# Squares of the input norm on other engines, high parts of softmax weights on ScalarE, and state space blocks moved by other transfers, in a one-core decoder trunk

## The chip, the core and the metric

The kernel runs on one core of a Trainium2 chip. The core has a matrix engine (TensorE, PE in the rows; its weight loads are PEld), VectorE (DVE), ScalarE (ACT), GpSimd (POOL), and SyncE (SP), which in this kernel issues every transfer. Each engine works through its own list of instructions in the order in which the program was built; an instruction that waits holds up all that stands behind it on that engine.

The metric is the device time of one execution in microseconds. Before the change it is 2130.84 us, the median of 3 runs (2130.14 to 2133.14).

## The reference, cut to what matters

```python
def layer(x, mem):                        # x: 1024 tokens x 1024 channels, float32
    h = rmsnorm(x, norm_mix)
    fq, fk, fv, ff, su, hq, hf, hi, hg, gl = split(h @ w_in)
    y_fox = fox_attention(q, k, v, log_f)     # 8 heads x 64, causal softmax with a forget bias
    y_s5  = s5_mixer(su, ...)                 # 32 groups x 16 channels, 64 complex states each,
                                              # gelu, then z * sigmoid(z @ w_glu + b_glu)
    y_hg  = hgrn2_mixer(hq, hf, hi, hg)       # 4 heads, chunks of 64
    merged = sum(sigmoid(gl)[b] * (y_b @ w_branch[b]) for y_b in (y_fox, y_s5, y_hg))
    x = x + merged @ w_out
    x = x + cross_attention(rmsnorm(x), rmsnorm(mem))    # 4 heads, 256 memory tokens
    x = x + swiglu(rmsnorm(x))
```

## The kernel before

Activations lie transposed: channels on the 128 partitions, the 1024 tokens along the row. A float32 product is made of three float32r matmuls: each operand is split into a high part (`xh`, `wh`, `yh`, `zh`, made by ScalarE) and the low remainder (`xl`, `wl`, `yl`, `zl`, made by VectorE), and PE runs high x high, low x high, high x low. A block of weights is loaded raw (`wr`), split into `wh` and `wl`, and used for one projection of 1024 tokens (two halves of 512, PSUM tile `pj`).

The stages, in the order of time:

- Start (0 to about 60 us). `load_x` loads the eight blocks `xk` of x, splits them into `xh` and `xl` and sums their squares for the input norm: blocks with an even number are squared on ScalarE and added on VectorE (`acc`), blocks with an odd number are squared and added on GpSimd (`accg`, which shows as `sq` in the rows). `run` meanwhile feeds PE with the projections `su0` and `su1`; one VectorE instruction merges `accg` into `acc`, and `row_scale` sums over the partitions on PE (`rs`). The outputs `su0` to `su3` are the input of the state space part; `su_evac` scales them and stores each to `su_d` in HBM.
- S5 (about 95 to 320 us). Eight blocks `o` of four groups. `s5_prep` loads a block's input as `s5u`, `s5_prep2` and `s5_body` build the operands (`kcs`, written by VectorE, is the last one) and run the matmuls (`s5y`), `s5_out` applies the gelu and stores to `sz_d`. `s5_main` runs the four steps for different blocks in turn; between two steps a planner puts projection matmuls (`pj`) on PE, `S5_W[lag] * S5_US` microseconds of them by its own count.
- FoX (about 320 to 600 us). Sixteen units (head pair `p`, half of the queries, head `h`). For each key block `j`, PE makes scores `st`, ScalarE the exponentials `pf`, GpSimd their high part `pt` (first half of the tile) and the running sum `facc`, VectorE the low part `pt` (second half), PE the product with the values `pv`. `fox_pre` prepares the next unit in between: the row maxima `mx`, and from them in `chain` the tile `mc` (GpSimd copies a constant into it, VectorE writes the two columns of the maxima), which `rows` transposes on PE (`mt`). When both heads of a pair have ended, `sums` splits `facc` into `ah` and sums it on PE (`sm`). `later(us, fn)` puts it that many planned microseconds of PE behind.
- HGRN2 (about 600 to 980 us), then the merge. For each branch, `gates(b, y)` multiplies eight output blocks by a gate that comes back from HBM (`gate`, from `gz_d`). First gate stage 0 (FoX), while the last HGRN2 head ends (`hoT`, stored to `hy_d`); then `glu` (the product z @ w_glu, on `zt`, loaded from `sz_d`, split into `zh` and `zl`); then `gates(1)` (S5) and `gates(2)` (HGRN2, whose inputs `load_parts` reads back from `hy_d` as `ldy` and splits into `yh` and `yl`).
- Output projection, cross attention and SwiGLU follow; the change does not touch them.

What sets the order: every instruction gets a rising priority when the program is written, and the scheduler orders each engine's list by it and by dependence. `ahead(n, fn)` gives the instructions of `fn` a priority that is n steps earlier. `drive` and `pump` write projection matmuls between the steps of a stage. Tiles such as `gate`, `wr`, `zt` and `ldy` come from one arena of equal slots, and a load waits until a slot is free.

Of the kernel before, what the change touches and what calls it, by code (L numbers as in the profile page):

```python
# [10 lines left out]
F32 = mybir.dt.float32  # L11
# [42 lines left out]
S5_W = (1.0, 0.6, 1.0, 1.2)  # L54
# [19 lines left out]
MIX_US = 8.5  # L74
EPS = 1e-6
# [118 lines left out]
class Trunk:  # L194
# [280 lines left out]
    def load_x(self):  # L475

        nc = self.nc
        self.xh = [self.u(f"xh{k}", F32R) for k in range(KB)]
        self.xl = [self.u(f"xl{k}", F32R) for k in range(KB)]
        acc, accg = self.u("acc"), self.u("sq")  # L480
# [4 lines left out]
        def square(k, xk):  # L485
            if k % 2 == 0:
                self.sq_add(xk, acc, k, eng=nc.vector)
                return
            sq = accg if k == 1 else self.u("sq")
            self.mul(sq, xk, xk, nc.gpsimd)  # L490
            if k > 1:
                self.add(accg, accg, sq, nc.gpsimd)

        last = None
        for k in range(KB):
            xk = self.u("xk")
            cuts = [slice(0, NT)] if k else [slice(0, 512), slice(512, NT)]
            if k == 0:
                nc.sync.dma_start(out=raw[:, 0:2], in_=ap[:, 0:2])
            for c in cuts:  # L500
                nc.sync.dma_start(out=xk[:, c], in_=self.io["xT"][k][:, c])
            if k == 0:
                nc.sync.dma_start(out=raw[:, 2:], in_=ap[:, 2:])
                self.w_load(1)
                self.split(raw[:, 0:2], hi[:, 0:2], lo[:, 0:2])
            for c in cuts:
                self.split_gain(xk[:, c], self.par("norm_mix", k), self.xh[k][:, c], self.xl[k][:, c])
            if k == 0:
                self.split(raw[:, 2:], hi[:, 2:], lo[:, 2:])
                del self.wraw[0]  # L510
                self.w_prep(1)
            else:
                square(k - 1, last)
            last = xk
        self.w_load(2)
        square(KB - 1, last)
        return acc, accg

# [164 lines left out]
    def fox_pre(self, un):  # L683
# [32 lines left out]
        def chain():  # L716
# [3 lines left out]
            mc = self.sp.tile([P, 4, 16], F32, tag="mc", name="mc")  # L720
            mh = self.sp.tile([P, 4], F32R, tag="mh", name="mh")
            self.nc.gpsimd.tensor_copy(out=mc, in_=self.ohc[:, hd].unsqueeze(1).to_broadcast([P, 4, 16]))
# [3 lines left out]
            st["mc"] = mc  # L726
# [11 lines left out]
        return out + [chain, rows]  # L738

    hi_pool = (0, 1, 2, 3)  # L740

    def fox_main(self):
# [11 lines left out]
        for ui, un in enumerate(units):  # L754
# [17 lines left out]
            for j in range(nj):  # L772
# [12 lines left out]
                if j % 4 in self.hi_pool:  # L785
                    self.ts(pt[:, 0, q0:512], pr, 1.0, 0.0, ALU.mult, ALU.add, self.nc.gpsimd)
                else:
                    self.act(pt[:, 0, q0:512], pr, AF.Copy)
# [29 lines left out]
    def fox_out(self, un, o, acc):  # L818
# [26 lines left out]
        if h == 1:  # L845
            self.later(2.0, sums)
# [31 lines left out]
    def su_evac(self, i):  # L878
        st = {}

        def f(ps, c, last):
# [7 lines left out]
            self.nc.sync.dma_start(out=self.su_d[128 * i:128 * i + 128], in_=t)  # L889
# [205 lines left out]
    def s5_prep(self, o):  # L1095
# [108 lines left out]
    def s5_out(self, o):  # L1204
# [21 lines left out]
        qv = q.rearrange("p (g c) -> p g c", g=4)  # L1226
# [103 lines left out]
    def run(self, stop=None):  # L1330
        nc = self.nc
        self.su_d = self.dp.tile([512, 8, 128], F32, name="su_d")
        self.fy_d = self.dp.tile([4, P, NT], F32, name="fy_d")
        self.hy_d = self.dp.tile([4, P, NT], F32, name="hy_d")
        self.sz_d = self.dp.tile([512, 8, 128], F32, name="sz_d")
# [16 lines left out]
        xs = acc = accg = None  # L1352
# [988 lines left out]
```

## Time and profile before

| | |
|---|---|
| median of 3 runs | 2130.84 us |
| the profiled execution's own time | 2138.17 us |
| its span on the core | 2136.1 us |
| mean granted TensorE clock | 0.992 |
| PE busy | 2079.2 us (97% of the span) |
| VectorE busy | 1521.9 us (71%) |
| ScalarE busy | 814.8 us (38%) |
| GpSimd busy | 608.2 us (28%) |

The profile is of one execution. Its rows come in a few views: the page (busy times of the engines, the chain that ended last), the waits of an engine, groups of instructions by line, a timeline of an engine (start in us, duration in us, line, what it did, and in brackets the idle time ahead and whose result ended it), and windows (busy times and the mean granted clock of PE in a stretch; 1.00 is 2.4 GHz, 0.50 is 1.2 GHz).

### The profile page before, as it was taken

What the parts mean: (1) busy time and instruction counts of PE and PEld (TensorE: products, weight loads), DVE (VectorE), ACT (ScalarE), POOL (GpSimd) and SP (SyncE); (2) the same over time, 40 slices, a digit from 0 to 9 for tenths busy, and PEclk for the clock granted to TensorE, in tenths of its full rate; (3) what the DMA queues carried; (4) which work ended last, traced back from release to release, by engine and by line L of the source; (5) the groups of instructions that cost most, each with busy time, mean ns of one, the idle gap of its engine ahead of it and who ended that gap; (6) DMA issues with size and microseconds to landing.
All of it is one profiled execution on the core that took longest, in us unless ns stands there. A gap on an engine that the chain in (4) does not pass through costs nothing.

```text
span 2136.1 us, 26862 instructions
## 1 busy us (share of the span) xinstructions
PE 2079.2 (97%) x10044; PEld 1706.7 (80%) x10044; DVE 1521.9 (71%) x2229; ACT 814.8 (38%) x1268; POOL 608.2 (28%) x551
## 2 busy tenths in 40 slices
PE   7998999999999999999999999999999999999999
PEld 5887777776788878888778888878788888888887
DVE  8887898888854566545675567656897778775772
ACT  4113345545531123215434445444533333344441
POOL 4281204454543223221722100011032324221320
PEclk9999999999999999999999999999999999999999
DMA  4332221110213233235554523334232322248582
GB/s 163 137 104 74 51 75 32 40 50 30 70 46 124 73 109 123 74 99 196 194 192 154 201 92 106 119 117 135 74 120 98 124 99 99 103 150 282 189 281 99
DMA packets 121042, 250.94 MB, mean 117 GB/s; under 512 B 15816, under 2 KB 53704, under 8 KB 120912
## 3 DMA queue, kind: packets, MB, share of 16 engines
q1 hardware_dynamic: 120912, 249.23, 34.2%
q8 instruction: 79, 1.29, 0.3%
q14 instruction: 51, 0.42, 0.1%
HBM read 184.83 MB, written 63.18 MB: 116 GB/s over the span
## 4 chain that ended last, share of the span: by engine, by line
PE 59%; DVE 4%; DMA 1%; ACT 1%; issue 0%; SPq 0%; DVEq 0%; ACTq 0%
PE fp L228 27%; PE pj L228 26%; PE hs L228 2%; PE xo L228 1%; PE xs L228 1%; PE rs L228 1%; PE ho L228 0%; DVE t L246 0%; DVE tl L246 0%; DVE gate L246 0%; DMA gate<-gz_d 0%; DVE yl L246 0%; DMA wr<-xv 0%; DMA ldy<-hy_d 0%; PE xt L233 0%
## 5 line engine op out<-in xcount | busy, mean ns | idle before, releaser
L228 PE MATMUL pj<-xl,wh 128*128 128x512 f32 x784 | 315.5, 406 | 4.7 <-DVE xl L258 4.6
L228 PE MATMUL pj<-xh,wh 128*128 128x512 f32 x784 | 313.3, 405 | 6.7 <-ACT xh L243 5.8
L228 PE MATMUL pj<-xh,wl 128*128 128x512 f32 x784 | 311.7, 401 | 0.0
L246 DVE TENSOR_TENSOR wl<-wr,wh 128x1024 fp32r<-128x1024 f32 (+2 forms) x138 | 170.4, 1236 | 58.5 <-ACT wh L243 56.2
L228 PE MATMUL fp<-th,wc 128*128 128x512 f32 x640 | 206.9, 389 | 0.0
L228 PE MATMUL fp<-hh,wc 128*128 128x512 f32 x644 | 191.4, 389 | 0.0
L228 PEld LDWEIGHTS pj<-xh,wh 128*128 128x128 f32 x784 | 149.2, 190 | 40.0 <-ACT xh L243 6.1
L228 PEld LDWEIGHTS pj<-xl,wh 128*128 128x128 f32 x784 | 148.5, 190 | 37.4 <-DVE xl L258 7.1
L228 PEld LDWEIGHTS pj<-xh,wl 128*128 128x128 f32 x784 | 149.1, 190 | 30.8 <-issue 1.9
L228 PE MATMUL fp<-fx,wc 128*128 128x512 f32 x720 | 172.9, 389 | 0.0
L243 ACT ACTIVATE wh<-wr 128x1024 fp32r<-128x1024 f32 (+2 forms) x138 | 131.8, 957 | 76.8 <-DMA wr<-w_in 50.3
L228 PEld LDWEIGHTS fp<-fx,wc 128*128 128x128 f32 x720 | 135.2, 188 | 28.0
L228 PEld LDWEIGHTS fp<-hh,wc 128*128 128x128 f32 x644 | 120.9, 188 | 25.0
L228 PEld LDWEIGHTS fp<-th,wc 128*128 128x128 f32 x640 | 120.2, 188 | 24.9
L246 DVE TENSOR_TENSOR wc<-wr,wc 128x512 fp32r<-128x512 f32 (+1 forms) x116 | 108.5, 954 | 31.4 <-ACT wc L243 31.4
L246 POOL TENSOR_TENSOR dm<-dm 128x256 f32<-128x256 f32 (+1 forms) x96 | 79.5, 828 | 179.9 <-DMA dm<-w_dn 163.0
L246 POOL TENSOR_TENSOR acc<-acc,sq 128x512 f32<-128x512 f32 (+1 forms) x18 | 30.7, 1706 | 340.5 <-ACT sq L243 340.4
L228 PE MATMUL fp<-tl,wc 128*128 128x512 f32 x320 | 124.6, 389 | 0.7 <-DVE tl L246 0.7
L246 DVE TENSOR_TENSOR pt<-pf,pt 128x512 fp32r<-128x512 f32 (+1 forms) x96 | 94.4, 985 | 40.2 <-POOL pt L262 39.9
L246 POOL TENSOR_TENSOR fc<-fc,fs 128x512 f32<-128x512 f32 x40 | 58.0, 1449 | 216.2 <-ACT fs L243 216.2
L228 PE MATMUL fp<-hl,wc 128*128 128x512 f32 x280 | 108.9, 389 | 0.0
L262 POOL TENSOR_SCALAR pt<-pf 128x512 fp32r<-128x512 f32 (+1 forms) x96 | 67.7, 706 | 139.0 <-ACT pf L243 127.8
(427 smaller groups left out, 4862.3 us busy)
## 6 DMA issues: line engine op xcount, KB each, us to landing
wr<-w_in SPq DMA_DIRECT2D x48, 512.0 KB, 4.8
wr<-w_gu SPq DMA_DIRECT2D x44, 512.0 KB, 4.1
hr<-hb_d SPq DMA_DIRECT2D x35, 512.0 KB, 5.4
hb_d<-fc SPq DMA_DIRECT2D x44, 256.0 KB, 2.1
gz_d<-gz SPq DMA_DIRECT2D x20, 512.0 KB, 2.9
dm<-w_dn SPq DMA_DIRECT2D x20, 512.0 KB, 5.6
ws_d<-dm SPq DMA_DIRECT2D x20, 512.0 KB, 3.3
gate<-gz_d SPq DMA_DIRECT2D x20, 512.0 KB, 6.4
```

The costliest lines, as they stand in the source:

```text
L228: self.nc.tensor.matmul(out, lhsT, rhs, start=start, stop=stop)
L243: self.nc.scalar.activation(out=out, in_=in_, func=f, **kw)
L246: return (eng or self.nc.vector).tensor_tensor(out=out, in0=a, in1=b, op=op)
L262: (eng or self.nc.vector).tensor_scalar(out=out, in0=a, scalar1=s1, scalar2=s2, op0=op0, **kw)
```

## The change

Five edits.

1. Input norm: all eight squares go to ScalarE, after all the splits, and the seven additions to VectorE behind the last `xl`. GpSimd has no part in it, and the merge is gone.
2. `su_d` and `sz_d` get another layout, by blocks. `s5_prep` loads a block with one transfer of 128 x 512 in place of eight, `s5_out` stores with one in place of eight. On the other sides `su_evac` stores with eight transfers in place of one (4 to 32 in all), and each `zt` is loaded with eight in place of one (4 to 32). In all SP issues 703 transfers in place of 759.
3. `S5_W`: the planner puts 1.6 in place of 1.0 of its units behind `s5_prep` and 0.6 in place of 1.2 behind `s5_out`.
4. FoX: the high part of all 96 exponentials is a ScalarE copy; the constant of `mc` is copied when a unit is built; `chain` is written with a priority 40 steps ahead; `sums` comes 6.0 in place of 2.0 planned microseconds later.
5. `load_parts` is stepped during `gates(1)`: the inputs of `gates(2)` are loaded and split between the gates of `gates(1)`.

PE runs the same 9467 instructions.

```diff
-S5_W = (1.0, 0.6, 1.0, 1.2)
+S5_W = (1.6, 0.6, 1.0, 0.6)
+SUM_AT = 6.0
+AH_MAX = 40
@@ load_x
-            else:
-                square(k - 1, last)
-            last = xk
         self.w_load(2)
-        square(KB - 1, last)
-        return acc, accg
+        for k, xk in enumerate(xs):
+            self.sq_add(xk, acc, k, eng=nc.vector)
+        return acc
@@ fox_pre, build
+            mc = st["mc"] = self.sp.tile([P, 4, 16], F32, tag="mc", name="mc")
+            self.nc.gpsimd.tensor_copy(out=mc, in_=self.ohc[:, hd].unsqueeze(1).to_broadcast([P, 4, 16]))
@@ fox_pre, chain
-            self.nc.gpsimd.tensor_copy(out=mc, in_=self.ohc[:, hd].unsqueeze(1).to_broadcast([P, 4, 16]))
@@ fox_pre, end
-        return out + [chain, rows]
-    hi_pool = (0, 1, 2, 3)
+        return out + [lambda: self.ahead(AH_MAX, chain), rows]
@@ fox_main
-                if j % 4 in self.hi_pool:
-                    self.ts(pt[:, 0, q0:512], pr, 1.0, 0.0, ALU.mult, ALU.add, self.nc.gpsimd)
-                else:
-                    self.act(pt[:, 0, q0:512], pr, AF.Copy)
+                self.act(pt[:, 0, q0:512], pr, AF.Copy)
@@ sums
-            self.later(2.0, sums)
+            self.later(SUM_AT, sums)
@@ su_evac
-            self.nc.sync.dma_start(out=self.su_d[128 * i:128 * i + 128], in_=t)
+            for n in range(8):
+                self.nc.sync.dma_start(out=self.su_d[2 * i + n // 4][:, :, n % 4].rearrange("s h c -> h s c"),
+                                       in_=t[16 * n:16 * n + 16])
@@ s5_prep
-        for s in range(8):
-            nc.sync.dma_start(out=U[16 * s:16 * s + 16],
-                              in_=self.su_d[64 * o:64 * o + 64, s].rearrange("(g h) c -> h g c", g=4))
+        nc.sync.dma_start(out=ut[:, 0:512], in_=self.su_d[o].rearrange("s h g c -> (s h) (g c)"))
@@ s5_out
-        for t in range(8):
-            nc.sync.dma_start(out=self.sz_d[64 * o:64 * o + 64, t].rearrange("(g h) c -> h g c", g=4),
-                              in_=qv[16 * t:16 * t + 16])
+        nc.sync.dma_start(out=self.sz_d[o].rearrange("t h g c -> (t h) (g c)"), in_=q)
@@ run
-                self.stt(acc, accg, 1.0 / 1024.0, acc, ALU.mult, ALU.add)
@@ run, loads of zt
-            self.nc.sync.dma_start(out=z, in_=self.sz_d[128 * i:128 * i + 128].rearrange("p t c -> p (t c)"))
+            zv = z.rearrange("p (t c) -> p t c", t=8)
+            for n in range(8):
+                self.nc.sync.dma_start(out=zv[16 * n:16 * n + 16],
+                                       in_=self.sz_d[2 * i + n // 4][:, :, n % 4].rearrange("t h c -> h t c"))
@@ run, gates
-        self.filler("gate1", self.gates(1, ys))
+        yh = []
+        self.filler("gate1", self.gates(1, ys, self.load_parts([self.hy_d[h] for h in range(4)], yh)))
-        self.filler("gate2", self.gates(2, self.load_parts([self.hy_d[h] for h in range(4)])))
+        self.filler("gate2", self.gates(2, yh))
@@ gates
             yield from self.gate(b, ob, y)
+            if side is not None:
+                next(side, None)
```

Where the order of the engines' lists differs. First VectorE at the start, before the change, from the split of the third last block of x on (`xl` is the low part of x, `acc` the sum of squares):

```order
L258 SCALAR_TENSOR_TENSOR xl_91<-xk,parT,xh_83 128x1024
L246 TENSOR_TENSOR acc<-acc,sq 128x1024
L258 SCALAR_TENSOR_TENSOR xl_92<-xk,parT,xh_84 128x1024
L258 SCALAR_TENSOR_TENSOR xl_93<-xk,parT,xh_85 128x1024
L246 TENSOR_TENSOR acc<-acc,sq 128x1024
L258 SCALAR_TENSOR_TENSOR acc<-sq,acc 128x1024
L441 CAST crr<-cr 128x384
L246 TENSOR_TENSOR wl<-wr,wh 128x1024
L258 SCALAR_TENSOR_TENSOR acc<-rs,cst,acc 128x512
```

The same place on VectorE after the change:

```order
L260 SCALAR_TENSOR_TENSOR xl_91<-xk,parT,xh_83 128x1024
L260 SCALAR_TENSOR_TENSOR xl_92<-xk,parT,xh_84 128x1024
L260 SCALAR_TENSOR_TENSOR xl_93<-xk,parT,xh_85 128x1024
L248 TENSOR_TENSOR acc<-acc,sq 128x1024 x6
L443 CAST crr<-cr 128x384
L248 TENSOR_TENSOR acc<-acc,sq 128x1024
L248 TENSOR_TENSOR wl<-wr,wh 128x1024
L260 SCALAR_TENSOR_TENSOR acc<-rs,cst,acc 128x512
```

The additions that stood between the splits stand behind them, and there are seven in place of three and a merge.

PE at the end of a FoX head pair, before the change (the place of the sums `sm` at 508.6 to 512.2 us in the timeline; the last `pv` of the pair are 128 wide):

```order
L228 MATMUL pv<-pt,vs 128x128
L228 MATMUL pj<-xh_83,wh 128x512
L228 MATMUL pj<-xl_91,wh 128x512
L228 MATMUL pj<-xh_83,wl 128x512
L228 MATMUL pj<-xh_84,wh 128x512
L228 MATMUL pj<-xl_92,wh 128x512
L228 MATMUL pj<-xh_84,wl 128x512
L228 MATMUL pj<-xh_85,wh 128x512
L228 MATMUL pj<-xl_93,wh 128x512
L228 MATMUL pj<-xh_85,wl 128x512
L228 MATMUL pj<-xh_78,wh 128x512
L228 MATMUL sm<-ah,crr 8x512 x3
```

The end of the same stretch on PE after the change, with the sums behind the first products and row maxima of the next unit:

```order
L230 MATMUL st<-q12a,k_2332 128x512
L230 MATMUL pj<-xl_86,wh 128x512
L230 MATMUL pv<-pt,vs 128x512
L230 MATMUL pj<-xh_78,wl 128x512
L230 MATMUL pj<-xh_79,wh 128x512
L230 MATMUL pv<-pt,vs 128x512
L230 MATMUL mx<-k_2333,qmm 128x512
L230 MATMUL pj<-xl_87,wh 128x512
L230 MATMUL pj<-xh_79,wl 128x512
L230 MATMUL mx<-k_2333,qmm 128x128
L230 MATMUL mx<-crr 128x128
L230 MATMUL mx<-k_2333,qmm 128x512
L230 MATMUL sm<-ah,crr 8x512 x4
```

The sums moved down by the rest of a projection's rows, four `pv` and the first row maxima.

SP ahead of the GLU, before the change (`zt` is the input of the GLU, `w_glu` its weights, `hoT` the last HGRN2 head, `gate` the gates of stage 0, `dm` and `ws_d` a staging of later weights):

```order
L1395 DMA zt<-sz_d 128x1024 x4
L1646 DMA gate<-gz_d 128x1024
L351 DMA wr<-w_glu 128x512
L2220 DMA dm<-w_dn 128x4x128
L1646 DMA gate<-gz_d 128x1024
L351 DMA wr<-w_glu 128x512
L1608 DMA hy_d<-hoT 128x1024
L2218 DMA ws_d<-dm 128x4x128
L351 DMA wr<-w_glu 128x512 x2
```

The same place on SP after the change:

```order
L2207 DMA dm<-w_dn 128x4x128
L1378 DMA zt<-sz_d 16x8x128 x32
L1593 DMA hy_d<-hoT 128x1024
L1631 DMA gate<-gz_d 128x1024
L353 DMA wr<-w_glu 128x512
L2205 DMA ws_d<-dm 128x4x128
L1631 DMA gate<-gz_d 128x1024
L353 DMA wr<-w_glu 128x512 x2
L2207 DMA dm<-w_dn 128x4x256
L353 DMA wr<-w_glu 128x512
```

The last two gates of stage 0 and the first two blocks of `w_glu` stood ahead of the store of `hoT` and stand behind it.

## Rows read from the trace of the kernel before

**Rows 1.** The page: busy time, share of the span and instructions of each engine, and the chain that ended last by engine.
```profile
PE 2079.2 (97%) x10044; PEld 1706.7 (80%) x10044; DVE 1521.9 (71%) x2229; ACT 814.8 (38%) x1268; POOL 608.2 (28%) x551
PE 59%; DVE 4%; DMA 1%; ACT 1%; issue 0%; SPq 0%; DVEq 0%; ACTq 0%
```

**Rows 2.** The waits of PE over the whole span: for whose result, us in total, times, longest us.
```profile
PE s5y L228 <- DVE kcs L246: 10.1, 6, 3.3
PE sm L228 <- DVE ah L246: 8.0, 5, 2.3
PE mt L233 <- DVE mc L246: 7.9, 9, 1.7
```

**Rows 3.** Timeline of PE at the start, at the `xl` blocks: start, us, what, and the wait ahead.
```profile
16.62 1.08 PE L228 MATMUL pj<-xh,wh 128*128 128x512 f32 x4
19.35 1.07 PE L228 MATMUL pj<-xh,wh 128*128 128x512 f32 x4
...
26.67 0.73 PE L228 MATMUL pj<-xl,wh 128*128 128x512 f32 x2 [3.09 <-DVE xl L258]
34.04 0.73 PE L228 MATMUL pj<-xl,wh 128*128 128x512 f32 x2 [1.52 <-DVE xl L258]
38.73 1.45 PE L228 MATMUL rs<-acc,cst 128*128 128x512 f32 x3
```

**Rows 4.** Timelines of VectorE, GpSimd and ScalarE at the start.
```profile
23.24 6.20 DVE L258 SCALAR_TENSOR_TENSOR xl<-xk,parT,xh 128x1024 fp32r<-128x1024 f32 x2
32.71 2.47 DVE L258 SCALAR_TENSOR_TENSOR xl<-xk,parT,xh 128x1024 fp32r<-128x1024 f32 x2
28.44 3.26 POOL L246 TENSOR_TENSOR sq<-sq 128x1024 f32<-128x1024 f32 x1
18.82 2.17 ACT L243 ACTIVATE xh<-xk,parT 128x1024 fp32r<-128x1024 f32 x2
20.89 1.04 ACT L243 ACTIVATE sq<-xk 128x1024 f32<-128x1024 f32 x1
```

**Rows 5.** Timelines of SP's queue (the issue of transfers), ScalarE and PE: one transfer, groups of eight, the weights behind the stores of `su_d`, their split, and PE's first matmul with them.
```profile
53.66 0.33 SPq L889 DMA_DIRECT2D su_d<-su  x1
160.32 3.61 SPq L1228 DMA_DIRECT2D sz_d<-s5u  x8
188.63 7.03 SPq L1105 DMA_DIRECT2D s5u<-su_d  x8
51.54 0.89 SPq L351 DMA_DIRECT2D wr<-w_in  x2
58.15 1.06 ACT L243 ACTIVATE wh<-wr 128x1024 fp32r<-128x1024 f32 x1 [13.78 <-DMA wr<-w_in]
62.37 0.39 PE L228 MATMUL pj<-xh,wh 128*128 128x512 f32 x1
```

**Rows 6.** S5: timeline of PE at two waits, and windows of 4 us behind them (start and end, length, busy us and instructions of PE, PEld, VectorE, ScalarE, GpSimd, granted clock, share of the DMA engines, GB/s).
```profile
168.80 0.80 PE L228 MATMUL s5y<-kcs,s5x 128*128 128x128 f32 x2 [2.62 <-DVE kcs L246]
206.93 0.80 PE L228 MATMUL s5y<-kcs,s5x 128*128 128x128 f32 x2 [3.34 <-DVE kcs L246]
208.00:212.00 4.00, 4.00 (x16) 3.61 (x16) 2.32 (x8) 0.51 (x1) 0.00 (x0) 0.50 0.06 13
```

**Rows 7.** FoX: groups of instructions of 325 to 600 us by line and shape (busy us, mean ns, idle ahead and its releasers), the window of this stretch (columns as in rows 6), one low part on VectorE with GpSimd idle, and the longest wait of the sums.
```profile
L246 DVE TENSOR_TENSOR pt<-pf,pt 128x512 fp32r<-128x512 f32 x43 | 53.9, 1256 | 24.2 <-POOL pt L262 24.0
L262 POOL TENSOR_SCALAR pt<-pf 128x512 fp32r<-128x512 f32 x43 | 32.0, 747 | 57.5 <-ACT pf L243 51.7 <-DVE pt L246 2.3 <-DVE ah L246 2.2
L246 POOL TENSOR_TENSOR facc<-facc,pf 128x512 f32<-128x512 f32 x21 | 30.9, 1469 | 4.6 <-ACT pf L243 4.6
L243 ACT ACTIVATE pf<-st 128x512 f32<-128x512 f32 x43 | 25.4, 597 | 44.5 <-PE st L228 36.6 <-DVE pt L246 5.4 <-DVE fy L246 1.4
325.00:600.00 275.00, 255.66 (x1229) 200.54 (x1229) 231.31 (x367) 147.72 (x248) 137.35 (x168) 0.99 0.12 43
326.16 0.69 DVE L246 TENSOR_TENSOR pt<-pf,pt 128x512 fp32r<-128x512 f32 x1 [0.80 <-POOL pt L262]
512.22 0.40 PE L228 MATMUL sm<-ah,crr 128*8 128x512 f32 x1 [2.26 <-DVE ah L246]
```

**Rows 8.** Ahead of the GLU: timelines of SP's queue, VectorE and PE, and from the page the median us from issue to landing of a gate.
```profile
966.24 2.28 SPq L1395 DMA_DIRECT2D zt<-sz_d  x4
995.39 0.33 SPq L1608 DMA_DIRECT2D hy_d<-hoT  x1
994.11 1.22 DVE L246 TENSOR_TENSOR hoT<-hoT,hgg 128x1024 f32<-128x1024 f32 x1
998.51 0.62 PE L228 MATMUL pj<-zh,wh 128*128 128x512 f32 x2
gate<-gz_d SPq DMA_DIRECT2D x20, 512.0 KB, 6.4
```

**Rows 9.** The start of `gates(2)`: timeline of PE and of SP's queue, and windows of 4 us (columns as in rows 6).
```profile
1050.17 2.18 SPq L1685 DMA_DIRECT2D ldy<-hy_d  x4
1071.06 0.79 PE L228 MATMUL pj<-yl,wh 128*128 128x512 f32 x1 [3.94 <-DVE yl L246]
1068.00:1072.00 4.00, 0.94 (x2) 0.83 (x3) 4.00 (x3) 0.00 (x0) 4.00 (x2) 0.72 0.00 0
1072.00:1076.00 4.00, 4.00 (x11) 3.05 (x10) 2.05 (x2) 0.00 (x0) 3.77 (x5) 0.50 0.02 4
```

More of the change, by code (lines that the diff above doesn't have):

```diff
@@ L479, in load_x @@
         self.xl = [self.u(f"xl{k}", F32R) for k in range(KB)]
-        acc, accg = self.u("acc"), self.u("sq")
+        acc = self.u("acc")
         _, ap, shape = self.wlist[0]
@@ L483, in load_x @@
         self.wraw[0], self.wrdy[0] = raw, (hi, lo)
[L485 to L494, printed above, removed]
+        xs = []
         for k in range(KB):
             xk = self.u("xk")
+            xs.append(xk)
             cuts = [slice(0, NT)] if k else [slice(0, 512), slice(512, NT)]
@@ L719, in chain @@
                 self.nc.vector.tensor_reduce(out=mn, in_=st["pm"], axis=AX.X, op=ALU.max, negate=True)
-            mc = self.sp.tile([P, 4, 16], F32, tag="mc", name="mc")
+            mc = st["mc"]
             mh = self.sp.tile([P, 4], F32R, tag="mh", name="mh")
-            self.nc.gpsimd.tensor_copy(out=mc, in_=self.ohc[:, hd].unsqueeze(1).to_broadcast([P, 4, 16]))
             self.nc.vector.tensor_copy(out=mh, in_=mn)
@@ L725, in chain @@
             self.sub(mc[:, :, 9], mn, mh.bitcast(F32))
-            st["mc"] = mc
         def rows():
@@ L1225, in s5_out @@
         self.mul(q, q, y)
-        qv = q.rearrange("p (g c) -> p g c", g=4)
-        for t in range(8):
-            nc.sync.dma_start(out=self.sz_d[64 * o:64 * o + 64, t].rearrange("(g h) c -> h g c", g=4),
-                              in_=qv[16 * t:16 * t + 16])
+        nc.sync.dma_start(out=self.sz_d[o].rearrange("t h g c -> (t h) (g c)"), in_=q)
     def s5_main(self):
@@ L1331, in run @@
         nc = self.nc
-        self.su_d = self.dp.tile([512, 8, 128], F32, name="su_d")
+        self.su_d = self.dp.tile([8, 8, 16, 4, 128], F32, name="su_d")
         self.fy_d = self.dp.tile([4, P, NT], F32, name="fy_d")
         self.hy_d = self.dp.tile([4, P, NT], F32, name="hy_d")
-        self.sz_d = self.dp.tile([512, 8, 128], F32, name="sz_d")
+        self.sz_d = self.dp.tile([8, 8, 16, 4, 128], F32, name="sz_d")
         self.gz_d = self.dp.tile([24, P, NT], F32, name="gz_d")
@@ L1341, in run @@
         self.plan_rest()
-        xs = self.load_x()
+        acc = self.load_x()
         self.setup2()
@@ L1346, in run @@
             if k == 3:
-                acc, accg = xs
-                self.stt(acc, accg, 1.0 / 1024.0, acc, ALU.mult, ALU.add)
                 self.Rb = self.row_scale(acc)
@@ L1351, in run @@
                 self.later(8.0, lambda: self.col_scale(self.Rb, self.Rt, 8))
-        xs = acc = accg = None
+        acc = None
         self.filler("su", self.su_projs())
@@ L1655, in merge_split, with gates @@
         self.mg[ob] = (mh, ml)
-    def gates(self, b, y):
+    def gates(self, b, y, side=None):
         for ob in range(8):
             yield from self.gate(b, ob, y)
+            if side is not None:
+                next(side, None)
     def glu(self, zt, y):
@@ L1679, in glu, with load_parts @@
             yield from self.proj(f"glu{i}", lambda k: zs[k], ev(i), nk=4)
-    def load_parts(self, srcs):
-        out = []
+    def load_parts(self, srcs, out):
         for s in srcs:
@@ L1685, in load_parts @@
             self.nc.sync.dma_start(out=t, in_=s)
+            yield
             h, l = self.u("yh", F32R), self.u("yl", F32R)
@@ L1688, in load_parts @@
             out.append((h, l))
-        return out
+            yield
     def residual(self, name, rhs, src, gain, keep=None, nwide=1, ready=None):
```

## The prediction

> **What bounds the kernel now.** I read the page first: PE is busy for 97% of the span and holds most of the chain that ended last [rows 1]. PE runs the same 9467 matmuls after the change, so time can come only from two places: the 57 us in which PE is idle (2136.1 less 2079.2), and stretches in which its clock is granted at 1.2 GHz after a wait. So the next view is the list of PE's waits. Its first three lines are the change's targets: `s5y` waits for `kcs`, `sm` for `ah`, `mt` for `mc`, 26.0 us together [rows 2]. Then come the timelines at the start, where PE waits twice for `xl` [rows 3], and at the start of `gates(2)`, where it waits 3.94 us for `yl` [rows 9]. The windows show what a wait costs beyond itself: the clock is 0.50 for 4 us after the waits at 206.93 and at 1071.06, which is 2.0 us of lost work each [rows 6, 9]. What I look for in each stage is which engine ends the wait last, and what would be last if it did not.
>
> All sums are made against the profiled execution (span 2136.1 us, own time 2138.17). The median of the runs is 2130.84, 7.3 us lower, so I carry only the difference over.
>
> **Start: about -4.** PE takes 2.73 us for a block of x (19.35 less 16.62), so from 16.62 the six blocks left would end at 33.0; `rs` starts at 38.73 [rows 3]. 4.6 us of the 5.7 are the two waits for `xl`. While GpSimd multiplies and adds (its last operation ends at 31.7), an `xl` takes 3.10 us on VectorE; right after, 1.23 us [rows 4]. The change takes GpSimd away and puts the additions behind the `xl`, so the `xl` come every 1.23 us, well inside PE's 2.73. The sum of squares is late in its place: the last `xh` ends by 20.99 at the latest, eight squares at 1.04 make 29.3, the last addition 30.5 [rows 4]. PE asks for it at 33.0, so it is hidden with 2.5 us to spare. Gain 5.7, at least 4.6.
>
> Against it stands the new store of `su_d`. Before, one store holds SP for 0.33 us; groups of eight small transfers hold it for 3.61 to 7.03, that is 0.45 to 0.88 a transfer [rows 5]. Two groups now stand ahead of the weights that were issued at 51.54. At 0.45, starting 5.7 us earlier (about 42), they end at 49.4 and the weights go out at about 50.5, only 1 us earlier than before, while PE wants them 5.7 earlier. Before, `wh` was made at 59.2 and PE used it at 62.37 [rows 5], 3.1 to spare. So 5.7 - 1.0 - 3.1 = 1.6 us of new wait (0 to 3). Net -4, from -2 to -5.7.
>
> **S5: about -8.** The numbers in `S5_W` move filler from behind `s5_out` to behind `s5_prep`, that is between a block's input and its `kcs`. I counted from the order how much PE work stands ahead of each block's first `s5y` and how much VectorE work ahead of `kcs`; PE's lead grows by 0.6 to 7.6 us in all eight blocks. For the two longest waits, 2.62 and 3.34 [rows 6], it grows by 1.9 and 0.6, which leaves 0.7 and 2.7; the other four, 4.1 us together (10.1 less 5.96 [rows 2, 6]), have 2.2 to 3.1 each and vanish. That is 6.6, and about 1.5 of the clock's 2 us behind such waits. The single transfers also take 3 to 7 us per block off SP, ahead of the weights [rows 5]; they were mostly in time, so I count nothing. From 0 to -13: nothing if VectorE, nearly always busy here, merely meets PE later, and -13 if waits and low clock all go.
>
> **FoX: about -8.** Three edits. The sums: PE work between a pair's last `pv` and `sm` rises from 2.2 to 4.0 us to 5.5 to 7.6 us (the order of PE in the change section, at 0.23 us a matmul); the longest wait is 2.3 [rows 2, 7], so all 8.0 go. `mt`, 7.9 us [rows 2]: the change means the chain to come ahead, but in VectorE's order the chain's rows hardly move; what stands between the last row maximum and `mc` adds up to 23.0 us over the sixteen units before, 24.8 after. I count 0 (from -5 to +2). The copies: a 512-wide copy is near an exponential of the same width, 0.60 us, against 0.75 on GpSimd [rows 7], so the path to `pv` gets no longer. With the narrower ones that is some 41 us more on ScalarE, 189 of 275 us in place of 147.7. It is still less loaded than VectorE with 231 [rows 7], but exponentials now queue behind copies: +0 to +4, I take 0. Sum -8, from -13 to +4.
>
> A 512-wide low part takes VectorE 1.26 us on average, and 0.69 where GpSimd is idle [rows 7]: 24 us over the 43. The Trainium skill (SBUF — State Buffer, section "Who interferes with whom") says that a VectorE instruction with two SBUF inputs and a GpSimd instruction that reads SBUF exclude each other, and the later one waits for the whole of the other. By it the copies that leave GpSimd free VectorE of up to 24 us, and the `facc` additions, 1.47 us each, still block it; the trace's 0.69 against 1.26 agrees, and by it FoX would come nearer to -13 than to 0.
>
> **Ahead of the GLU: about +8.** This is the term against the change. SP waits at the store of `hoT`, since `hoT` is finished at 995.3 (994.11 + 1.22) [rows 8]. Before, the last two gates of stage 0 and two blocks of `w_glu` had been issued ahead of it; now they stand behind it. `hoT` itself comes a VectorE row (0.7 us) earlier. So, in the times of before: hoT 994.6, store issued, first gate issued 995.0, landed 6.4 us later [rows 8] at 1001.4; the second some 1.3 us later at 1002.7. ScalarE works in order: sigmoid, `wh`, second sigmoid (1.05) to 1003.8, then the first `zh` (1.0) to 1004.8. PE wants it at 998.51 [rows 8]: 6.3 us of wait, and about 2 of low clock, as after 1071. From +4 (the gates land in 4 us) to +11.
>
> **gates(2): about -7.** The 3.94 us and the low clock around it (0.50 in one window [rows 9], near 1 us on both sides) come from four loads issued together at 1050.17 and four splits behind them. Stepped through `gates(1)`, the splits lie on VectorE between gates. From -4 to -7. What hides this is free slots of the arena in `gates(1)`; without one, SP waits at an `ldy` with gates and weights behind it.
>
> **Sum:** -4 - 8 - 8 + 8 - 7 = -19: span 2117, median 2112.
>
> **Rivals.**
> 1. *The gates land in time, or `mt` gains too:* the GLU term falls to +4, and S5 or `mt` gives 4 more. -27, median 2104. For it: the GLU's wait rests on a median landing time, when SP has little else in flight. Against: ScalarE's order makes both gates precede `zh`. Chance 0.14.
> 2. *VectorE keeps the waits:* in S5 and FoX PE merely meets VectorE elsewhere, since VectorE has 231 of 275 us in FoX. S5 and FoX give 0: -4 + 8 - 7 = -3, median 2128. Against: the waits are few and at fixed places, and they get more cover there. Chance 0.13.
> 3. *Small transfers at the upper price:* at 0.88 us each (7.03 for eight [rows 5]) the two groups at the start end at 56 in place of 49.4 (+6), and the 32 of `zt` hold SP for 28 us in place of 14; issued from 966 on they reach past `hoT`'s 995 with the rest behind them (+6). -7, median 2124. It decides from about 0.8 us a transfer. Chance 0.07. The Trainium skill (DMA: Bandwidth & Descriptors, section "Rules for kernel authors") wants small transfers merged, since under 64 KB they are mostly overhead; `su_evac` and `zt` now do the opposite with 64 KB pieces. The rows' 0.45 to 0.88 us a transfer on SP is what speaks to it; none shows 64 KB pieces.
> 4. *ScalarE bounds FoX (slower):* exponential and copy stand in one queue, and each score tile's PSUM is free only when its exponential has run. Each copy that is exposed costs its own 0.27 to 0.6 us, 41 in all. The change turns slower once over 23 of the 41 us are exposed; with 30 exposed, -19 + 30 = +11, median 2142. For it: ScalarE also carries the splits of q, k and weights, in bursts. Against: 69% load. Chance 0.08.
>
> That the change doesn't do what it says holds for one edit only, the row maxima, and is in the forecast.
>
> **How the numbers follow.** Forecast 2112, chance 0.58, by itself 2103 to 2121. A measurement of this kernel can tell about 0.2%, 4.3 us. Faster: nearly all of the forecast (0.56), rival 1 (0.14), most of rival 3 (0.05) and some of rival 2 (0.05): 0.80. Same: 0.02 + 0.02 + 0.06: 0.10. Slower: rival 4 and the end of rival 2: 0.10. The range, 2101 to 2127, leaves out rival 4, about half of rival 2 and the far end of rival 1.
>
> **What would show it.** Start: no wait for `xl`, `rs` near 33, a wait for `wh` of 1 to 3 us near 56. S5: waits for `kcs` of some 3.5 in place of 10.1 us. FoX: no line `sm` from `ah`, `mt` from `mc` near 8 us, `st` or `pv` from ScalarE under 4. GLU: a new line `pj` from `zh`, 4 to 7 us, with SP waiting at the `hoT` store right before. `gates(2)`: no wait for `yl`. Wrong would be the forecast if waits of PE for ScalarE in FoX sum to over 10 us, or if `pj` from `zh` is missing or over 12.

## The result and the profile after

The changed kernel takes 2152.77 us (median of 4 runs, 2149.66 to 2155.66) against 2131.99 us (4 runs) of the kernel before: ratio 1.0097, 95% interval 1.0077 to 1.0117. It is about 21 us slower, where 19 us faster was forecast, and lies outside the range.

The page of the changed kernel, busy times and the chain by engine [rows 1]:

```profile
PE 2084.5 (97%) x10044; PEld 1713.2 (80%) x10044; DVE 1498.8 (70%) x2232; ACT 863.5 (40%) x1367; POOL 537.4 (25%) x448
PE 71%; DVE 6%; ACT 2%; issue 1%; DMA 1%; SPq 0%; DVEq 0%; ACTq 0%
```

PE is as busy as before, so the loss is again waits and low clock: 68.0 us idle (2152.5 less 2084.5) against 56.9, and a mean granted clock of 0.987 against 0.992. PE's waits after the change [rows 2] (for whose result, us in total, times, longest):

```profile
PE s5y L230 <- DVE kcs L248: 14.2, 5, 5.0
PE pj L230 <- DVE wl L248: 9.1, 6, 3.7
PE mt L235 <- DVE mc L248: 7.7, 5, 4.8
...
PE pj L230 <- ACT zh L245: 4.0, 1, 4.0
PE pv L230 <- DVE pt L248: 3.4, 4, 2.1
PE mx L230 <- DVE pmx L705: 3.2, 1, 3.2
PE hst L230 <- ACT hbT L245: 3.0, 1, 3.0
...
PE sm L230 <- DVE ah L248: 1.6, 1, 1.6
```

`sm` fell from 8.0 to 1.6 and the lines of `xl` and `yl` are gone, as meant. But `kcs` rose from 10.1 to 14.2, and five lines are new or much longer. To place them I compared stages by PE's timeline, from the start of one marker instruction to the start of another (us):

| stage, from and to | before | after | difference |
|---|---|---|---|
| start: 0 to `rs` | 38.73 | 30.84 | -7.9 |
| `rs` to the first transpose `ct` | 10.01 | 10.01 | 0.0 |
| `ct` to the first row maximum `mx` (weights behind the start, and S5) | 268.41 | 285.14 | +16.7, 5.2 of it work moved ahead of the marker |
| first `mx` to the first `hs` (FoX) | 348.25 | 349.68 | +1.4, so +6.6 for equal work |
| first `hs` to the last `hst` (HGRN2) | 306.59 | 308.77 | +2.2 |
| last `hst` to the last `zh` product (merge, GLU) | 48.50 | 58.40 | +9.9 |
| last `zh` product to the first `xs` (rest of the merge, output projection) | 233.93 | 227.78 | -6.2 |

They add up to 16.2 us, the difference of the first `xs` (1254.42 to 1270.62) and of the two spans within 0.2; nothing behind the merge moved. The medians are 21 us apart: the profiled execution of the kernel before lies some 6 us above its median, that of the changed kernel 2 us, so the table leaves out some 4 us of the loss.

Start and weights behind it, timelines of PE, SP and VectorE after the change [rows 3 to 5]:

```profile
30.84 1.88 PE L230 MATMUL rs<-acc,cst 128*128 128x512 f32 x4
56.23 0.50 PE L230 MATMUL pj<-xh,wh 128*128 128x512 f32 x1 [0.90 <-ACT wh L245]
72.41 0.80 PE L230 MATMUL pj<-xh,wl 128*128 128x512 f32 x1 [3.72 <-DVE wl L248]
...
40.20 7.47 SPq L876 DMA_DIRECT2D su_d<-su  x16
49.67 7.04 SPq L876 DMA_DIRECT2D su_d<-su  x8
...
56.21 1.23 DVE L248 TENSOR_TENSOR wl<-wr,wh 128x1024 fp32r<-128x1024 f32 x1 [9.53 <-ACT wh L245]
71.14 1.22 DVE L248 TENSOR_TENSOR wl<-wr,wh 128x1024 fp32r<-128x1024 f32 x1
```

The norm came 7.9 us earlier. After it the stores of `su_d` hold SP, the weights come late, and VectorE idles 9.5 us at `wl`; the S5 parameters that stand behind it slip, and with them the next `wl`, for which PE waits 3.72 us at 72.41.

S5, timelines of VectorE, GpSimd and PE after the change, at the two long waits [rows 6]:

```profile
169.04 3.01 DVE L1179 TENSOR_TENSOR_SCAN s5dd<-s5rv,s5dd 128x128 f32<-128x128 f32 x4
173.69 3.12 DVE L248 TENSOR_TENSOR s5dd<-s5dd,s5e 64x508 f32<-64x508 f32 x2
229.23 4.53 DVE L1179 TENSOR_TENSOR_SCAN s5dd<-s5rv,s5dd 128x128 f32<-128x128 f32 x4
301.22 1.36 DVE L1179 TENSOR_TENSOR_SCAN s5dd<-s5rv,s5dd 128x128 f32<-128x128 f32 x4
...
169.37 1.26 POOL L248 TENSOR_TENSOR s5x<-s5pw,s5bx 128x512 f32<-128x512 f32 x1 [21.71 <-PE pj L230]
229.80 1.18 POOL L248 TENSOR_TENSOR s5x<-s5pw,s5cx 128x512 f32<-128x512 f32 x1
...
178.92 0.79 PE L230 MATMUL s5y<-kcs,s5x 128*128 128x128 f32 x2 [4.96 <-DVE kcs L248]
238.68 0.80 PE L230 MATMUL s5y<-kcs,s5x 128*128 128x128 f32 x2 [5.03 <-DVE kcs L248]
```

The same scan takes 1.36 us with GpSimd idle (301.22) and 3.01 and 4.53 us while GpSimd computes the products of `s5_prep` for a later block. At the first long wait the scan and the two `s5dd` rows behind it (3.12 against 1.38 elsewhere) lose 3.4 of the 4.96 us; at the second the scan alone loses 3.2 of 5.03.

The kernel before has such meetings too, two of its eight scans (2.12 us at 140.9 and 2.22 at 200.4), the second ahead of its longest wait, at 206.93 (timelines of VectorE and GpSimd before):

```profile
164.09 1.36 DVE L1193 TENSOR_TENSOR_SCAN s5dd<-s5rv,s5dd 128x128 f32<-128x128 f32 x4
200.44 2.22 DVE L1193 TENSOR_TENSOR_SCAN s5dd<-s5rv,s5dd 128x128 f32<-128x128 f32 x4
...
200.04 1.39 POOL L246 TENSOR_TENSOR s5tm<-s5rv,s5bx 128x512 f32<-128x512 f32 x1
```

FoX and the start of HGRN2, rows of VectorE, GpSimd and PE after the change [rows 7]:

```profile
L248 DVE TENSOR_TENSOR pt<-pf,pt 128x512 fp32r<-128x512 f32 x40 | 39.2, 983 | 16.9 <-ACT pt L245 16.5
...
448.80 4.98 POOL L248 TENSOR_TENSOR facc<-facc,pf 128x512 f32<-128x512 f32 x3 [3.76 <-ACT pf L245]
450.87 1.78 DVE L260 SCALAR_TENSOR_TENSOR ry<-sq,ry 128x512 f32<-128x512 f32 x1
452.57 1.75 DVE L248 TENSOR_TENSOR pt<-pf,pt 128x512 fp32r<-128x512 f32 x1
...
332.02 1.02 PE L235 MATMUL mt<-cst,mc 128*16 128x128 f32 x4 [4.76 <-DVE mc L248]
424.19 0.90 PE L230 MATMUL pv<-pt,vs 128*128 128x256 f32 x3 [2.07 <-DVE pt L248]
456.17 0.44 PE L230 MATMUL mx<-k,qmm 128*128 128x384 f32 x1 [3.23 <-DVE pmx L705]
756.77 0.94 PE L230 MATMUL hst<-hv,hbT 128*128 128x128 f32 x6 [2.96 <-ACT hbT L245]
```

The low parts `pt` fell from 1.26 to 0.98 us, still above 0.69; the `facc` additions stay on GpSimd, and the row at 452.57 runs beside three of them. Where `sm` waited before, `pv`, `mx` and later `hst` wait now.

Ahead of the GLU, timelines of SP, ScalarE and PE after the change [rows 8]:

```profile
979.66 17.91 SPq L1378 DMA_DIRECT2D zt<-sz_d  x31
1008.01 0.34 SPq L1593 DMA_DIRECT2D hy_d<-hoT  x1
...
1013.10 1.06 ACT L245 ACTIVATE gate<-gate 128x1024 f32<-128x1024 f32 x1 [8.03 <-DMA gate<-gz_d]
1015.88 1.06 ACT L245 ACTIVATE gate<-gate 128x1024 f32<-128x1024 f32 x1 [1.20 <-DMA gate<-gz_d]
...
1017.93 1.22 PE L230 MATMUL pj<-zh,wh 128*128 128x512 f32 x2 [4.03 <-ACT zh L245]
```

This is the sequence of the forecast: SP past the store of `hoT` at 1008.0, gate landed at 1013.1, PE waits 4.03 us for `zh`.

### The profile page after: what moved, and what is told of

Its sections match the earlier page's. It is cut to its first block, busy times and chain, and to the rows that moved or that the text cites. A ratio compares the mean times of both kernels' runs of the same rounds, so it can differ in the third digit from the quotient of the medians.

```text
span 2152.5 us, 26896 instructions
## 1 busy us (share of the span) xinstructions
PE 2084.5 (97%) x10044; PEld 1713.2 (80%) x10044; DVE 1498.8 (70%) x2232; ACT 863.5 (40%) x1367; POOL 537.4 (25%) x448
## 4 chain that ended last, share of the span: by engine, by line
PE 71%; DVE 6%; ACT 2%; issue 1%; DMA 1%; SPq 0%; DVEq 0%; ACTq 0%
PE pj L230 35%; PE fp L230 27%; PE hs L230 2%; PE st L230 1%; PE rs L230 1%; PE xo L230 1%; PE pv L230 1%; PE xs L230 1%; PE ho L230 1%; PE mx L230 1%; DVE t L248 0%; DVE ry L260 0%; DVE tl L248 0%; ACT sq L245 0%; ACT wh L245 0%
## 5 line engine op out<-in xcount | busy, mean ns | idle before, releaser
L248 POOL TENSOR_TENSOR dm<-dm 128x256 f32<-128x256 f32 (+1 forms) x96 | 88.8, 925 | 160.7 <-DMA dm<-w_dn 133.4
L248 POOL TENSOR_TENSOR facc<-facc,pf 128x256 f32<-128x256 f32 (+1 forms) x64 | 70.9, 1107 | 119.0 <-ACT pf L245 113.2
L248 DVE TENSOR_TENSOR pt<-pf,pt 128x512 fp32r<-128x512 f32 (+1 forms) x96 | 72.8, 760 | 38.2 <-ACT pt L245 37.8
```

Of the source, the lines that this page charges most:

```text
L248: return (eng or self.nc.vector).tensor_tensor(out=out, in0=a, in1=b, op=op)
```

## The experiments

The runs are called e1 to e11. All ratios are to the kernel before, run on the same chip (e9 to e11 ran on another chip than e1 to e8), with the 95% interval; 0.0010 is 2.1 us. Two runs are compared by these ratios; by their intervals a difference under some 3 to 5 us is not clear of noise. Each edit is made on the changed kernel (1.0097) unless another kernel is named.

**Undoing one edit in the changed kernel.** First the transfers:

```diff
-            for n in range(8):
-                self.nc.sync.dma_start(out=self.su_d[2 * i + n // 4][:, :, n % 4]..., in_=t[16 * n:16 * n + 16])
+            self.nc.sync.dma_start(out=self.su_d[128 * i:128 * i + 128], in_=t)
...
+        for s in range(8):
+            nc.sync.dma_start(out=U[16 * s:16 * s + 16], in_=self.su_d[64 * o:64 * o + 64, s]...)
```

> The changed kernel (2152.8 us) with the transfers of su_d and sz_d as before (one store for each su block and one load for each zt, eight transfers for each S5 block); all else as changed. Theory A (the small transfers on the two other sides cost: at the start they hold SP ahead of weights, about 5.5 us of waits for wh and wl near 56 and 72 us; at the GLU the hy_d store holds two gates back, 9.9 us): about 15 us less, 2137 us, with no wait for zh and none for wl near 72 us. Theory B (they cost nothing of their own; PE meets VectorE later anyway): 2148 to 2153 us.

Measured (e1): 1.0054 (1.0037 to 1.0071), 9 us less than the changed kernel. The waits for `zh` and for `wl` at 72 us are gone, and the GLU stage is back at 48.90 us. But from `ct` to `mx` it takes 286.38 us, no less than the changed kernel: a scan now takes 5.12 us and another 2.87, and PE waits 3.96 us for a `wl` at 315.8. Theory A's signs are there, its size only in part (9 of 15 us): what it gives is partly taken back in S5.

```diff
-S5_W = (1.6, 0.6, 1.0, 0.6)
+S5_W = (1.0, 0.6, 1.0, 1.2)
```

> The changed kernel with the old S5_W (1.0, 0.6, 1.0, 1.2); all else as changed. Theory A (the new numbers put GpSimd's six products of s5_prep beside VectorE's scan and kcs instructions of another block, which slows these: the scan 3.0 and 4.5 us in place of 1.4): 6 to 10 us less, 2143 to 2147 us, with no scan over 2.3 us. Theory B (the lost time in S5 comes from the start, where the planner's count and the engines have drifted apart through the small transfers): within 2 us of 2152.8, and the long scans stay.

Measured (e2): 1.0056 (1.0038 to 1.0074), 9 us less. The size is theory A's, but the sign of theory A is missing: the scans of 2.22 and 4.54 us are there with the old numbers too. From `ct` to `mx` it takes 281.94 us. So the new numbers are not needed for the collisions: with the new transfers and the old numbers they are there as well.

```diff
-                self.act(pt[:, 0, q0:512], pr, AF.Copy)
+                self.ts(pt[:, 0, q0:512], pr, 1.0, 0.0, ALU.mult, ALU.add, self.nc.gpsimd)
```

> The changed kernel with the high parts of the exponentials on GpSimd again; the rest of the FoX edits stays. Theory A (ScalarE's copies delay exponentials and q12, so pv and st wait): 4 to 7 us less in 320 to 620 us, 2146 to 2149 us, and the waits of pv for pt go. Theory B (the copies are paid for by a freer VectorE, and the FoX loss is from the order of chain and sums): the same or up to 6 us more, 2152 to 2159 us, with new waits of sm for ah.

Measured (e3): 1.0115 (1.0099 to 1.0131), 4 us more than the changed kernel, though the intervals overlap. Theory A is out: the copies on ScalarE are no loss, and rival 4 of the prediction falls (PE's waits for ScalarE's rows in FoX, `st` for `q12a` and `q12b` and `pv` for `pt`, sum to 3.1 us in the changed kernel). The time is theory B's; its sign, new waits of `sm` for `ah`, is missing (0.9 us).

**What the edits give on the kernel before.** The old transfers, old `S5_W` and the old FoX code, so that only the norm and the stepped `load_parts` are left:

```diff
         self.w_load(2)
+        for k, xk in enumerate(xs):
+            self.sq_add(xk, acc, k, eng=nc.vector)
...
+        self.filler("gate1", self.gates(1, ys, self.load_parts([self.hy_d[h] for h in range(4)], yh)))
```

> The kernel before with two of the five edits: the input norm's squares on ScalarE, and the loads and splits of gates(2) stepped through gates(1). Theory A (each edit gives what the changed kernel's own stage shows: rs 7.9 us earlier, gates(2) 6.1 us less, and nothing takes it back): 14 us less than before, 2118 us. Theory B (VectorE and the S5 chain take the start's gain back by 320 us): 6 us less, 2126 us.

Measured (e4): 0.9947 (0.993 to 0.9964), 11 us less than before. Nearer to theory A in size: `rs` comes 7.8 us earlier and by `mx` 10.4 us are won, so S5 takes nothing back (265.82 us from `ct` to `mx`). But A's second part, the gain of `gates(2)`, does not show in this kernel: last `zh` to first `xs` takes 234.50 us, since waits of 2.48 for `wl` and 2.59 for `wh` take the place of the one for `yl`.

**What GpSimd's products cost.** In `s5_prep` six fills stand in for the six products (the operands of S5, and so the output of the S5 branch, are left out):

```diff
-        self.mul(X, bh(self.prr), bk(bx[:, 0]), G)
-        self.mul(T, bh(self.pri), bk(bx[:, 1]), G)
-        self.add(X, X, T, G)
...
+        for v in (x_, t_, x_, z_, t_, z_):
+            G.memset(v, 0.01)
```

> The changed kernel, where GpSimd's six products of each s5_prep are replaced by fills of a constant of the same width, which read nothing (so the S5 operands, and with them the output of the S5 branch, are left out). Theory A (VectorE's scan and kcs instructions are slowed because GpSimd reads SBUF beside them): every scan takes 1.4 us, the waits of s5y for kcs fall from 14.2 to below 8 us, the first row maxima mx come 6 to 10 us earlier, and the time is 2143 to 2147 us. Theory B (the long waits come from the order: kcs is written late because of what stands ahead of it on VectorE): the waits for kcs stay above 11 us and the time within 3 us of 2152.8.

Measured (e5): 1.0007 (0.9996 to 1.0019), 19 us less than the changed kernel, twice what theory A expected. In the timeline of VectorE of this run every such scan is short, and PE's wait for `kcs` has almost gone:

```profile
170.47 1.37 DVE L1176 TENSOR_TENSOR_SCAN s5dd<-s5rv,s5dd 128x128 f32<-128x128 f32 x4
217.49 1.37 DVE L1176 TENSOR_TENSOR_SCAN s5dd<-s5rv,s5dd 128x128 f32<-128x128 f32 x4
```

```profile
PE s5y L230 <- DVE kcs L248: 2.7, 4, 1.1
```

From `ct` to `mx` it takes 267.46 us, 17.7 less than the changed kernel. The order of VectorE differs from the changed kernel's in a few rows here, fills are also shorter than products (0.53 us against 1.06 to 1.59), and no fill lies beside a scan, so the next run is its measure: the same edit in the kernel before.

> The kernel before, unchanged but for GpSimd's six products of each s5_prep, which are replaced by fills that read nothing (so the output of the S5 branch is left out). It sets the measure for e5, where the same took 19 us off the changed kernel. Theory A (in the kernel before GpSimd's products hit the chain to kcs once only, a scan of 2.2 us, so there is little to free): 2 to 5 us less than before. Theory B (the fills help any version alike, by freeing VectorE as a whole): 12 us or more less than before.

Measured (e11): 0.9976 (0.9965 to 0.9986), 5 us less than before: theory A, though two scans of the kernel before are slow and not one; the wait for `kcs` falls from 10.1 to 1.6 us, and `ct` to `mx` from 268.41 to 258.74 in its profile. By the ratios GpSimd's products cost the kernel before 5 us and the changed kernel 19. Without them the changed kernel is 1.0031 of the kernel before (1.0007 / 0.9976) in place of 1.0097: some 14 of the 21 us lost are this cost grown (9 to 19 by the intervals; 8 from `ct` to `mx` in the profiles, 17.7 less 9.7). In this run fills do run beside a scan and the rows behind it, and these keep their short durations (timelines of VectorE and GpSimd):

```profile
228.81 1.36 DVE L1187 TENSOR_TENSOR_SCAN s5dd<-s5rv,s5dd 128x128 f32<-128x128 f32 x4
230.91 1.38 DVE L248 TENSOR_TENSOR s5dd<-s5dd,s5e 64x508 f32<-64x508 f32 x2
229.40 1.94 POOL L1119 MEMSET s5x<- 128x512 f32 x4 [14.44 <-PE pj L230]
```

**The FoX edits, with S5 undisturbed.** Norm, `gates(2)` and all FoX edits on the old `S5_W` and transfers:

> The kernel before with the input norm, gates(2) and the FoX edits (old S5_W, old transfers), to be set against the run with the norm and gates(2) alone (0.9947 of before, 2123 us). Theory A (the FoX edits cost by themselves; ScalarE's queue and VectorE's order give new waits that outweigh the 8 us of sm): 3 to 7 us more than that run, 2126 to 2130 us. Theory B (in FoX of the changed kernel only the start was late, from the shifted S5; without the shift the edits gain): 3 to 8 us less, 2115 to 2120 us, no wait for mc over 2 us.

Measured (e6): 0.9971 (0.9956 to 0.9986), 5 us more than the norm and `gates(2)` alone: theory A. `sm` waits 1.6 and `mt` 3.1 us, but `pv` 3.4, `mx` 3.2 and `hst` 3.0 are there. The wait of 4.76 us for `mc` at the start of FoX is not. It goes with the new `S5_W`, and not with a late S5: the first `mt` waits little in e2, whose S5 is as late as the changed kernel's, and long in e5, whose first `mx` comes 16.7 us earlier (timelines of PE, e2 and then e5):

```profile
330.64 0.60 PE L235 MATMUL mt<-cst,mc 128*16 128x128 f32 x4 [0.19 <-DVE mc L248]
...
315.19 1.02 PE L235 MATMUL mt<-cst,mc 128*16 128x128 f32 x4 [3.73 <-DVE mc L248]
```

Between the first `mx` and the first `mt` PE runs 17 projection matmuls in the kernel before and in e2, 4 in e5 and none in the changed kernel: the new numbers put that work ahead of the first `mx`, and it was the cover of `mc`.

```diff
-        return out + [lambda: self.ahead(AH_MAX, chain), rows]
+        return out + [chain, rows]
```

> As the run e6, but with the chain to mc written as before (no priority ahead, the constant copied in the chain). Theory A (the chain's priority does nothing, since its rows hardly moved): within 2 us of e6. Theory B (it matters: mt waits less by it): 3 to 5 us more than e6, with mt from mc back at 7 to 8 us in place of about 4.

Measured (e7): 0.9974 (0.9963 to 0.9985). Theory A: the chain's priority does nothing that can be measured (`mt` waits 4.3 us).

With the high parts on GpSimd (the edit of e3, on the kernel of e6):

> As the run e6, but with the high parts of the exponentials on GpSimd as before. Theory A (the copies on ScalarE are a gain by themselves, as undoing them in the changed kernel made it 4 us slower): 3 to 8 us more than e6. Theory B (with the old S5 order GpSimd has room, and ScalarE's copies only queue): 0 to 4 us less than e6.

Measured (e8): 0.9987 (0.9977 to 0.9997), 3.4 us more than e6, between the ends of theory A. It agrees with e3, but each of the two differences is within its noise.

```diff
-SUM_AT = 6.0
+SUM_AT = 2.0
```

> The kernel before with the input norm, gates(2), ScalarE's copies and the chain ahead, but the sums at 2.0 planned us as before (old S5_W, old transfers). Theory A (the later sums are what costs: they push ah and the sums between the next unit's products, give pv and mx new waits of 3 us each, and shift ScalarE's order at the start of HGRN2, hbT 3.0 us): 8 to 12 us less than e6 (0.9971), 2116 to 2120 us, no wait of hst for hbT. Theory B (the later sums pay for themselves, 8 us of sm): 4 to 8 us more than e6, 2132 to 2136 us, with sm from ah back at 8 us.

Measured (e9): 0.993 (0.9917 to 0.9942), median 2118.41 us, 8.7 us less than e6 and the fastest kernel of the study: theory A. The waits of PE in this run:

```profile
PE mt L235 <- DVE mc L248: 5.8, 6, 1.6
...
PE sm L230 <- DVE ah L248: 2.2, 4, 1.0
```

`sm` does not go back to 8 us even at 2.0: the copies on ScalarE, not the later sums, are enough to bring it to 2.2 (3.6 with a wait of 1.4 for ScalarE's half of `ah`). No wait of `hst` for `hbT`, none of `mx` for `pmx`.

> The kernel before with the input norm, gates(2) and only the later sums (6.0) of the FoX edits; high parts on GpSimd, chain as before. Theory A: as e8 (0.9987, 2130 us), 8 us more than the run with norm and gates(2) alone (0.9947), with the wait of hst for hbT. Theory B: 4 to 8 us less than that run.

Measured (e10): 0.9974 (0.9964 to 0.9984), 5.8 us more than the norm and `gates(2)` alone: theory A again, a little below its size. The later sums, alone, bring the waits of `pv` (4.3 us), `mx` (3.2) and `hst` (3.0). This run differs from e7 (0.9974 too) only in the high parts on GpSimd: here ScalarE's copies gain nothing. That they cost nothing is shown; a gain of 3 to 4 us (e3, e8, and e9 against e4) is not clear of noise.

## Why the prediction was wrong, point by point

- **S5: -8 forecast; here the forecast broke.** From `ct` to `mx` the changed kernel takes 11.5 us more for equal work, some 7 of them at the late weights of the start. The step that failed is the count of PE's lead: so much PE work ahead of `s5y`, so much VectorE work ahead of `kcs`, with VectorE's instructions at fixed durations. The durations aren't fixed. They depend on what GpSimd does beside them, and the edits moved GpSimd's products onto the scan and the rows behind it: `kcs` 14.2 us in place of the forecast 3.5. VectorE is not slowed more on the whole (its busy time from `ct` to `mx` is 227.0 us, 234.3 before); it is slowed where PE waits for it. The waits of before were read in the same way: with fills alone, and PE's lead as it was, 8.5 of their 10.1 us go (e11). The prediction weighed GpSimd's reading against VectorE at the start and in FoX, and left it out in the one stage where VectorE's chain ends PE's wait. The runs with fills put some 14 us of the loss on GpSimd's products, where 8 us of gain were forecast. That it is what the products read, and not their length or the order, is shown for the rows above, not for each of these 14 us.
- **`S5_W` and the transfers do not add up.** With all FoX edits, norm and `gates(2)` in place, the transfers alone cost 1.0056 less 0.9971, about 18 us; the new `S5_W` alone 1.0054 less 0.9971, about 18; both 1.0097 less 0.9971, 27. Each of them alone brings the collisions (a scan of 4.54 in the one, of 5.12 in the other). Not every shift does: e4 and e6 to e10 start S5 4 to 8 us earlier than the kernel before and keep its two slow scans and its 10 us of waits for `kcs`. Why just these shifts meet GpSimd's products is only read from the traces, where a group starts once the tile it writes comes free. Of the new `S5_W`, 3 to 5 us are the wait for `mc` at the first `mt`, which no fill removes (3.73 in e5).
- **Start: -4 forecast.** `rs` 7.9 us earlier in place of 5.7, in the other kernels with this edit 4.4 to 7.8. The wait for `wh` came as said (0.90 and 0.53 us for `wl`), within 0 to 3. Missed was the second `wl` at 72.41, 3.72 us: I followed the late weights to their first matmul, and not VectorE's list behind the late `wl`. With the waits and a clock of 0.91 over 60 to 80 us some 7 us went again, so that about 1 us was left of the gain.
- **FoX: -8 forecast, about +7 measured in the changed kernel** (+6.6 for equal work). With the old `S5_W` the same edits leave this stretch about as it was, 346.8 us in e2 and 347.9 in e6 against 348.25; the rest of the +7 comes with the new `S5_W`, the wait of 4.76 us for `mc` first. Two of the three edits were read right: the chain does nothing, and the copies are no burden on ScalarE. The prediction thought that a GpSimd freed of the copies might bring FoX nearer to -13; the low parts on VectorE did get shorter, 1.26 to 0.98 us, but the times show no gain clear of noise. The step that failed is the sums: I counted the cover that `sm` gets and took the 8 us as won. Moved later, the sums and `ah` stand between the next unit's products, and `pv`, `mx` and `hst` wait instead; the edit costs 6 to 9 us (e10 against e4, e6 against e9). The wait went on, it did not end: PE idles for 19.4 us in this stretch in e4 and 19.9 in e10.
- **GLU: +8 forecast, +9.9 measured.** The mechanism was right in each step; the gates landed in about 4.3 us in place of the 6.4 assumed, so `zh` waits 4.03, and a wait of 2.50 for `wl`, which stands behind `hoT` on VectorE, comes on top, with a clock of 0.94 in this stage. With the old transfers the stage is back at 48.90 us.
- **`gates(2)`: -7 forecast, -6.2 measured** in the changed kernel, no wait for `yl`. It is not a gain of this edit by itself: the nine kernels with it and the later sums take 227.7 to 228.5 us for this stage, the two with it and the sums at 2.0 (e4 and e9) 234.50 and 233.79 us, as before (233.93), since PE then waits for weights. How the later sums help here was not tried, so that the forecast came near is in part luck. In e9 SP is held for 14.7 us at a staging transfer whose tile `dm` GpSimd has done only at 1057.1, with gates and weights behind it (timelines of SP and PE of that kernel):

```profile
1042.01 0.38 SPq L2207 DMA_DIRECT2D dm<-w_dn  x1
1057.09 0.38 SPq L2205 DMA_DIRECT2D ws_d<-dm  x1
...
1060.59 0.79 PE L230 MATMUL pj<-yh,wl 128*128 128x512 f32 x1 [2.47 <-DVE wl L248]
```

- **HGRN2: nothing forecast, +2.2 measured.** The wait of 2.96 for `hbT` comes with the later sums (all kernels with 6.0 have it, e4 and e9 do not). The +2.2 is too small a figure for them: the stage takes 306.7 us in the profile of the kernel before, 303.8 in e11, which has the same code here, 302.4 and 301.8 in e9 and e4, and 306.8 to 312.3 in the kernels with the later sums. By e10 less e4 and e6 less e9 the later sums cost 7 and 8 us here, where the prediction put nothing, and 3 and 6 in FoX, and 7 and 5 come back in the stage of `gates(2)`. The kernel before has a granted clock of 0.89 and 0.77 from 765 to 795 us with no wait ahead of it that the profile shows; in e4 it stays at 1.00 from 746 to 810 us. What decides this was not tried and stays open.
- **The rivals.** The slower side was to come from ScalarE in FoX; that rival was wrong in its place. Rival 2, that VectorE keeps the waits, was nearest in kind, but VectorE did not merely keep them: where PE waited for it, it got slower. Rival 3 turned on the price of a small transfer, 0.8 us and over: it was 0.47 us (16 in 7.47), 0.58 (31 in 17.91) and, for the eight at 49.67, 0.88, so it came true in one place of three. What the prediction called a sign of being wrong did not show, neither 10 us of waits for ScalarE in FoX nor a `zh` wait missing or over 12: both watched other stages than the one that broke; only its line on `kcs` (3.5 us) did.

A version without the two costly edits (transfers and `S5_W`) and without the later sums is e9: the norm, `gates(2)`, ScalarE's copies and the chain ahead, 15 us less than before.

## What to carry to other kernels

A VectorE instruction need not keep its duration while GpSimd works beside it (here a scan of 1.36 us took 4.53); before GpSimd work or the work beside it is moved in time, list what VectorE does in the new overlap, and first the chain that PE waits for. When a planner's numbers are changed, follow the instruction that waited to what now stands in its place: moving `sm` behind other work moved the wait to that work, and moving projection matmuls ahead of `mx` uncovered `mc`. A transfer pattern that is simpler on one side was paid for on the other here, and the price was where SP stood in front of something urgent: weights at the start, gates ahead of the GLU.

## What the runs showed of the hardware that was not expected

The scan (four instructions of 128 x 128) takes 1.36 us alone and up to 5.12 us beside GpSimd's two-input operations, more than three times as long; a pair of 64 x 508 products went from 1.38 to 3.12 us, a 128 x 512 scalar-tensor-tensor from 0.69 to 1.78 (beside `facc`). Fills on GpSimd, which read nothing, did not slow the one scan that had them beside it (e11, 1.36 us). The Trainium skill (SBUF — State Buffer, section "Who interferes with whom") says that a VectorE instruction with two SBUF inputs contends with a GpSimd instruction that reads SBUF and not with one that only writes it; these rows agree, the second half by that one scan and the rows behind it.
